# The value and gate projections of layer 1: sums of the next weights ahead of the remainder, one set of copies in smaller buffers, and the following stage's weights handled a product later

## The chip, the cores and the metric

The kernel runs on one core of one Trainium2 chip. The metric is the device time of one execution in microseconds (us). The core has engines that run side by side, each through its own list of instructions in order: TensorE (PE, matrix products), VectorE (DVE), ScalarE (ACT), GpSimd (POOL, hardly used here) and SyncE (SP, which issues nearly all DMA transfers). They wait for one another through semaphores. TensorE's granted clock over the profiled execution is 0.999 of full speed.

## The reference

What is computed is a trunk of two decoder layers on 1024 tokens of width 1024: layer 0 mixes tokens with dilated sliding-window attention, layer 1 with gated linear attention (GLA); each mixer is followed by a squared-ReLU MLP. The change lies in layer 1's mixer, of which this matters:

```python
def gla_mixer(h, w_in, w_gate_up, b_gate, norm_w, w_out):
    proj = h @ w_in
    ...
    q, k, v = proj[..., :s1], proj[..., s1:s2], proj[..., s2:s3]
    g_out, gate_lr = proj[..., s3:s4], proj[..., s4:]
    ...
    gate = jax.nn.silu(g_out.astype(jnp.float32)).reshape(B, S, GLA_HEADS, GLA_DV)
    o = (o * gate).reshape(B, S, GLA_VAL_DIM).astype(h.dtype)
    return o @ w_out
```

`v` and `g_out` are each a product of the normed activations (1024 x 1024) with 1024 columns of `w_in`. The stage in question computes these two products, group 0 being the gate `g_out` with its SiLU, group 1 the values `v`. The stage after it starts with the 16 columns of `gate_lr` and the heads' `k` and `q`.

## The kernel before

**Seven products.** Class `Values` computes a 1024 x 1024 x 1024 product by the Strassen-Winograd scheme: seven products of 512 x 512 blocks instead of eight, on sums and differences of blocks of the activations and of the weights. Each of the seven is done in two halves of 256 rows of the inner dimension. Steps are counted by `n`; for two groups there are 28: `place(n)` gives group g = n // 14, product q = (n % 14) // 2 and half m. "Product n" below is the half product of step n: 24 matmuls of 128 x 128 by 128 x 512 (two blocks of the inner dimension, four blocks of 128 tokens, and three terms). The three terms come from the precision: each operand is split into a rounded part `h` (made by ACT) and a remainder `l` (made by DVE as value minus rounded part), and h·h, h·l and l·h are summed.

**What one step needs.** For the weights of step n: `load(n)` issues a DMA on SP, into a tile named raw, or kept if a later step uses it again; `total(n)` (L784) forms the sum of blocks on DVE where the scheme wants one; `rounded(n)` (L808) is ACT's copy into `dh`; `remain(n)` (L814) is DVE's subtraction into `dl`; `prep(n)` is `rounded` and then `remain`, with `total` ahead where it hasn't been done. For the activations, `hs.sum1` to `hs.sum4` (L350) make sums of blocks on DVE, in two halves of columns c = 0, 1, and `hs.cut` splits them: L344 on ACT and L346 on DVE. `s1` to `s4` are these sums, `a11` to `a22` the blocks themselves.

**What is done with a product.** Products add up in PSUM, in two sets of four banks called A and B; a set that is used afresh (q = 0, 1, 2, 6) has to be free. `sums(n)` does the traffic: at q = 1, 3, 4 and 6 ACT copies the running sum out (`copy`: L896 for group 0, L839 for group 1), at q = 2, 5, 6 and at the next group's q = 0 DVE adds a bank to such a copy (`add`, L844), which finishes one quarter of the result, c11, c12, c21 or c22, each of four tiles t of 128 tokens. The fourth, c21, is copied from A at q = 6 (steps 12 and 13), just ahead of the adds of c22 that read the same banks. For group 1 a finished tile is stored at once (L900). For group 0 it goes on the list `todo`, and SiLU is applied to one tile per step: `begin` (L908, exp on ACT), in the next step `guard` (L913, DVE) and `logs` (L918 and L919, ACT), and in the step after that `close` (L925 to L927, DVE, and the store L928 on SP). `begin` starts at step 7; step 13 has none of the four.

**Buffers.** Tiles share rings by size: `k4`, twenty-five buffers of 4 KB per partition (weights, `dh`, `dl`, halves of the split s2, s3 and s4); `h8`, twelve of 8 KB (among others group 0's copies `gq`, four tiles in one buffer); `t2`, eight of 2 KB; eight PSUM banks. An instruction that takes a buffer waits until the last reader of what stood in it is done, and whatever is behind it on its engine waits too.

**Order.** The order on each engine is that of the calls in `gla_values` (L1729 to L1797), written out by hand for steps 0 to 3, then the loop over n = 4 to 27: first `guard` and `close`, then `sums(n)`, `prep(n + 2)`, loads, `product(n)`, extra cuts, `logs` and `begin`, and `total(n + 3)`.

**The next stage's weights.** They go through `W` (class `Weights`): `W.dma()` issues the next load (L135), `W.prep` splits one (L151 on ACT, L152 on DVE; the 16 columns of `gate_lr`, tile `wboth`, also L158), and `W.pump()` issues loads until four are ahead and prepares up to two of them, within `W.limit`. `plan_gla()` lists them, `wboth` first, at step 22. `wboth` is read by the first matmuls after the stage (L2010).

Of the kernel before, what the change touches and what calls it, by code (L numbers as in the profile page):

```python
# [9 lines left out]
F32 = mybir.dt.float32  # L10
# [3 lines left out]
AF = mybir.ActivationFunctionType  # L14
OP = mybir.AluOpType
# [4 lines left out]
P = 128  # L20
# [21 lines left out]
def hybrid_trunk(ctx, tc, x, norm_mix, norm_mlp, norm_fin, a_in, a_out, g_in, g_up, g_b, g_nw,  # L42
                 g_out, m_up, m_down, tab, msk, gmask, ident_d, out):
    nc = tc.nc
    pe, act, dve, pool, sp = nc.tensor, nc.scalar, nc.vector, nc.gpsimd, nc.sync
# [7 lines left out]
    def h8(shape, dt, name):  # L53
        return wk.tile(shape, dt, name=name, tag="h8", bufs=12)

    def k4(shape, dt, name):
        return wk.tile(shape, dt, name=name, tag="k4", bufs=25)

    def t2(shape, dt, name):
        return wk.tile(shape, dt, name=name, tag="t2", bufs=8)  # L60
# [50 lines left out]
    class Weights:  # L111
        def __init__(self):
            self.slots = []
            self.by = []
            self.ndma = 0
            self.nprep = 0
            self.used = 0
            self.freed = 0
            self.limit = 5
            self.second = dve  # L120
            self.parts = {}
            self.raws = {}
# [57 lines left out]
    W = Weights()  # L180
# [14 lines left out]
    def plan_gla():  # L195
        W.add(cols(g_in, 3072, RANK))
        for h in range(GH):
            add_two(g_in, 512 + DK * h, DK * h)
        for k in range(0, KT, 2):
            add_rows(g_out, k, lambda kt: gnw[:, kt % 2:kt % 2 + 1])  # L200
# [299 lines left out]
    class Up:  # L500
# [100 lines left out]
        def copy(self, p, name):  # L601
            e = t2([P, 512], F32, name)
            act.activation(e, self.st[p]["X"], AF.Copy)
            self.st[p][name] = e
# [273 lines left out]
    class Mixed(Values):  # L878
# [3 lines left out]

        def __init__(self):
            super().__init__()
            self.quad, self.todo, self.open, self.last = {}, deque(), None, None

        def source(self, g):
            return g_in, (2048, 1024)[g]
# [1 line left out]
        def copy(self, name, s, t, g):  # L890
            if g:
                return super().copy(name, s, t, g)
            if t == 0:
                self.quad[name] = h8([P, 4, 512], F32, "gq")
            c = self.c[name, t] = self.quad[name][:, t, :]
            act.activation(c, self.acc[s][t], AF.Copy)  # L896

        def made(self, c, g, rows, cols):
# [2 lines left out]
            else:  # L901
                self.todo.append((c, rows, cols))

        def begin(self):

            if self.todo:
                d = t2([P, 512], F32, "gd")
                act.activation(d, self.todo[0][0], AF.Exp, scale=-1.0)  # L908
                self.open = [*self.todo.popleft(), d]

        def guard(self):
            if self.open is not None:
                dve.tensor_scalar(self.open[3], self.open[3], 1.0, 3e38, op0=OP.add, op1=OP.min)  # L913

        def logs(self):
            if self.open is not None:
                e = t2([P, 512], F32, "ge")
                act.activation(e, self.open[3], AF.Ln)  # L918
                act.activation(e, e, AF.Exp, scale=-1.0)  # L919
                self.last, self.open = [*self.open, e], None  # L920

        def close(self):
            if self.last is not None:
                c, rows, cols, d, e = self.last
                dve.tensor_tensor(d, d, e, op=OP.mult)  # L925
                dve.scalar_tensor_tensor(e, d, 2.0, e, op0=OP.subtract, op1=OP.mult)
                dve.scalar_tensor_tensor(c, c, -1.0, e, op0=OP.mult, op1=OP.mult)  # L927
                sp.dma_start(ggscr[rows, cols], c)  # L928
                self.last = None


    clock = [0]
# [111 lines left out]
    class Heads(Up):  # L1044
# [92 lines left out]
        def follow(self, p, c, points):  # L1137
            h, g = divmod(p, NG)
            a = Attention(g, h, None, None)

            def begin():
                a.qT, a.kT = self.dst.pop((p, 0)), self.dst.pop((p, 1))
            at(c + points[0][0], begin, 0)
            a.plan(c, *points)
# [125 lines left out]
    for p in range(NB // 2):  # L1270
        t = h8([P, 2, D], F32, "x0")
# [9 lines left out]
    hs = Halves(x0, wbc, vals, None)  # L1281
# [117 lines left out]
    for p in range(heads.count):  # L1399
# [3 lines left out]
        if p == heads.count - 1:  # L1403
            for k in range(0, KT, 2):
                add_rows(a_out, k)
            c = 14 * p
# [322 lines left out]
    def gla_values():  # L1729

        hs, m = down.hs, down.mixed
        m.product(0)
        hs.turn(2)
        m.prep(3)
        m.load(4)
        m.product(1, [0, 1])
        m.product(1, [2, 3])
        hs.turn(3)
        m.load(5)
        hs.sum1(0)  # L1740
        hs.cut("s1", 0)
        m.sums(2)
        m.product(2)
        m.prep(4)
        hs.sum1(1)
        hs.cut("s1", 1)
        m.load(6)
        m.sums(3)
        m.product(3)
        m.prep(5)  # L1750
        for c in range(2):
            hs.sum2(c)
        hs.cut("s2", 0)
        m.load(7)
        m.total(6)
        for n in range(4, m.STEPS):
            if n != 13:
                m.guard()
                m.close()
            if n != 5:  # L1760
                m.sums(n)
            if n == 4:
                m.sums(5)
                hs.cut("s2", 1)
            m.prep(n + 2)
            m.load(n + (4 if n < 5 else 5))
            if n == 4:
                m.load(9)
            m.product(n)
            if n == 4:  # L1770
                hs.sum4()
                hs.cut("s4", 0)
            elif n == 5:
                hs.cut("s4", 1)
                hs.sum3()
                hs.cut("s3", 0)
            elif n == 6:
                hs.cut("s3", 1)
                hs.cut("a22", 0)
            elif n == 7:  # L1780
                hs.cut("a22", 1)
            if n != 13:
                m.logs()
                if n >= 7:
                    m.begin()
            if n + 3 < m.STEPS:
                m.total(n + 3)
            if n == 22:
                plan_gla()
                W.limit = 3  # L1790
            if n in (20, 21):
                hs.cut("a21", n - 20)
            if n >= 24:
                W.pump()
        for t in range(4):
            m.add("c21", "B", t, 1)
        return [[m.h["a11"], m.h["a12"]], [m.h["a21"], m.h["a22"]]]  # L1797
# [195 lines left out]

    ol, turn1 = [], []
    hT = gla_values()
    W.take(1)
    AM = k4([P, NB, P], F32, "AM")
# [21 lines left out]
    for h in range(GH):  # L2019
        rows = []  # L2020
# [55 lines left out]
```

## Time and profile before

| | |
|---|---|
| time, median of 3 runs | 2612.7 us (2612.32 to 2613.21) |
| time of the profiled execution | 2613.06 us |
| its span, first to last instruction | 2611.3 us |
| stage of the change in it (product 0 to the first matmul on `wboth`) | 1582.2 to 1743.7 us |

Engines in stretches of that stage, from the view of windows (busy us):

| stretch, us | length | PE | DVE | ACT |
|---|---|---|---|---|
| 1585 to 1618 | 33.0 | 33.00 | 28.53 | 18.45 |
| 1618 to 1636 | 18.0 | 16.09 | 15.71 | 11.12 |
| 1636 to 1662 | 26.0 | 26.00 | 22.74 | 13.51 |
| 1662 to 1700 | 38.0 | 37.82 | 35.52 | 26.02 |
| 1700 to 1745 | 45.0 | 43.82 | 37.36 | 23.58 |

How to read the lines that follow. A line of the timeline gives start and duration in us, engine, line of the kernel, operation, output <- inputs, sizes and count; in brackets stands the idle time of the engine before it and what ended that. A line of the list of waits gives the engine and line that waited, what it waited for, the total in us, how many times, and the longest. Matmuls overlap: each is listed with 0.39 us, while a new one starts every 0.22 to 0.23 us, so time that PE loses is read from the distance between starts.

### The profile page before, as it was taken

Reading aid. Unit: us, or ns where it says so; the run is one execution under the profiler, and the core shown is the slowest. Engines: PE = TensorE matmul, PEld = TensorE weight load, DVE = VectorE, ACT = ScalarE, POOL = GpSimd, SP = SyncE. Lnnn points to the kernel's source line nnn. Section 1 sums busy time; section 2 is a strip of 40 time slices with the busy share of each in tenths; the row PEclk is TensorE's granted clock in tenths of the full one; section 3 lists DMA queues with packets and bytes.
Section 4 is the critical chain, followed back from the end, with each engine's and each line's share of the span. In section 5 each row is a group of like instructions: output and inputs, shape, how many; then the busy total and the mean of one; then the engine's idle time right before and its main releaser. Section 6 shows DMA issues by size and latency. Waiting matters only on the chain.

```text
span 2611.3 us, 33042 instructions
## 1 busy us (share of the span) xinstructions
PE 2586.3 (99%) x12144; PEld 2157.3 (83%) x12144; DVE 1858.9 (71%) x2986; ACT 1276.7 (49%) x2319; POOL 1.8 (0%) x7
## 2 busy tenths in 40 slices
PE   8999999999999999999999999999999999999998
PEld 6888888888888888888888887878888888888887
DVE  7645888888888768666657577977658866666566
ACT  6332455555556446555533345654326545553343
POOL 0000000000000000000000000000000000000000
PEclk9999999999999999999999999999999999999999
DMA  5533465655556733454775452463513544396543
GB/s 190 169 129 124 103 161 131 163 147 150 155 151 183 227 121 128 167 169 137 283 252 185 137 194 93 133 199 97 187 66 123 170 153 157 131 355 200 189 146 125
DMA packets 327010, 423.12 MB, mean 162 GB/s; under 512 B 19808, under 2 KB 192224, under 8 KB 326848
## 3 DMA queue, kind: packets, MB, share of 16 engines
q1 hardware_dynamic: 326848, 421.01, 51.0%
q8 instruction: 95, 1.56, 0.3%
q14 instruction: 67, 0.55, 0.1%
HBM read 279.71 MB, written 116.06 MB: 152 GB/s over the span
## 4 chain that ended last, share of the span: by engine, by line
PE 87%; DVE 8%; ACT 3%; issue 1%; DMA 1%; SPq 0%; ACTq 0%; DVEq 0%
PE pX L598 16%; PE pB L1581 13%; PE pV L598 11%; PE pA L1581 10%; PE pY L598 5%; PE pZ L598 5%; PE pB L829 5%; PE pd L215 3%; PE pd L213 3%; PE pd L214 3%; PE pA L829 3%; PE pO L1017 2%; PE pS L976 2%; PE pP L1003 1%; DVE dl L814 1%
## 5 line engine op out<-in xcount | busy, mean ns | idle before, releaser
L1581 PE MATMUL pB<-dh 128*128 128x512 f32 x512 | 199.4, 389 | 0.0
L1581 PE MATMUL pB<-dh,dl 128*128 128x512 f32 x512 | 199.2, 389 | 0.0
L1581 PE MATMUL pB<-dl,dh 128*128 128x512 f32 x512 | 199.2, 389 | 0.0
L222 DVE TENSOR_TENSOR dl<-sin,dh 128x1024 fp32r<-128x1024 f32 x112 | 136.5, 1218 | 44.6 <-ACT dh L219 44.2
L219 ACT ACTIVATE dh<-sin 128x1024 fp32r<-128x1024 f32 x112 | 117.8, 1052 | 89.7 <-PE pB L1581 32.5
L219 ACT ACTIVATE dh<-kept 128x1024 fp32r<-128x1024 f32 x64 | 67.9, 1061 | 183.4 <-DVE kept L1546 137.8
L598 PE MATMUL pV<-s4h,wd 128*128 128x512 f32 x448 | 150.8, 398 | 0.0
L1581 PE MATMUL pA<-dh,dl 128*128 128x512 f32 x384 | 149.4, 389 | 0.0
L1581 PE MATMUL pA<-dl,dh 128*128 128x512 f32 x384 | 149.4, 389 | 0.0
L1581 PE MATMUL pA<-dh 128*128 128x512 f32 x384 | 149.4, 389 | 0.0
L992 ACT ACTIVATE pt<-pt,orow 128x128 f32<-128x128 f32 (+1 forms) x192 | 84.8, 443 | 96.7 <-DVE orow L990 94.6
L1581 PEld LDWEIGHTS pB<-dh,dl 128*128 128x128 f32 x512 | 96.1, 188 | 20.1
L1581 PEld LDWEIGHTS pB<-dh 128*128 128x128 f32 x512 | 96.1, 188 | 19.9
L1581 PEld LDWEIGHTS pB<-dl,dh 128*128 128x128 f32 x512 | 96.1, 188 | 19.8
L536 DVE TENSOR_TENSOR wal<-raw,wah 128x512 fp32r<-128x512 f32 x112 | 76.2, 686 | 42.9 <-ACT wah L535 42.9
L607 ACT ACTIVATE c<-c 128x512 f32<-128x512 f32 x64 | 40.4, 632 | 122.6 <-DVE c L635 78.9
L598 PEld LDWEIGHTS pV<-s4h,wd 128*128 128x128 f32 x448 | 84.2, 188 | 17.7 <-DVE rb L623 0.2
L222 DVE TENSOR_TENSOR dl<-kept,dh 128x1024 fp32r<-128x1024 f32 x64 | 78.3, 1224 | 25.1 <-ACT dh L219 19.3
L536 DVE TENSOR_TENSOR wbl<-t,wbh 128x1024 fp32r<-128x1024 f32 x56 | 68.6, 1225 | 38.3 <-ACT wbh L535 38.3
L990 DVE CUSTOM_DVE_ANT_0 pt<-pS,masks 128x128 f32<-128x128 f32 (+1 forms) x192 | 58.2, 347 | 51.2 <-PE pS L976 51.2
L598 PE MATMUL pY<-a12h,wah 128*128 128x512 f32 x224 | 89.5, 400 | 0.0
L598 PE MATMUL pZ<-a22h,wgh 128*128 128x512 f32 x224 | 89.3, 399 | 0.0
(336 smaller groups left out, 7364.2 us busy)
## 6 DMA issues: line engine op xcount, KB each, us to landing
sin<-acts SPq DMA_DIRECT2D x112, 512.0 KB, 3.8
raw<-in_mlp_w_up_dram SPq DMA_DIRECT2D x64, 512.0 KB, 6.0
acts<-s SPq DMA_DIRECT2D x64, 512.0 KB, 3.4
raw<-in_mlp_w_down_dram SPq DMA_DIRECT2D x64, 512.0 KB, 4.7
raw<-in_attn_w_in_dram SPq DMA_DIRECT2D x96, 256.0 KB, 4.6
cw<-c SPq DMA_DIRECT2D x192, 128.0 KB, 2.3
acts<-c SPq DMA_DIRECT2D x64, 256.0 KB, 2.1
kept<-in_mlp_w_down_dram SPq DMA_DIRECT2D x32, 512.0 KB, 5.8
```

The lines of the kernel that those rows point to most:

```text
L213: pe.matmul(ps, sh, mh, start=start, stop=False)
L214: pe.matmul(ps, sh, ml, start=False, stop=False)
L215: pe.matmul(ps, sl, mh, start=False, stop=stop)
L219: act.activation(hi, src, AF.Copy)
L222: dve.tensor_tensor(lo, src, hi.bitcast(F32), op=OP.subtract)
L536: self.remain(lambda: dve.tensor_tensor(lo, src, hi.bitcast(F32), op=OP.subtract))
L598: pe.matmul(st[b], u[:, k, :], v, start=first and k + n == 0, stop=k == 3 and n == 2, skip_group_check=True)
L829: pe.matmul(self.acc[s][t], a[:, c], b[:, k, :], start=fresh and m + k + v == 0, stop=m == 1 and k == 1 and v == 2, skip_group_check=True)
L976: pe.matmul(ps[:, i, :128 * n], self.qT[:, 128 * b:128 * b + 128], self.kT[:, k0:k0 + 128 * n], start=True, stop=True)
L990: dve.tensor_tensor_reduce(pt[:, i, :128 * n], ps[:, i, :128 * n], masks[:, m0:m0 + 128 * n], -scale, 1e38, op0=OP.add, op1=OP.min, accum_ ...
L992: act.activation(pt[:, i, :128 * n], pt[:, i, :128 * n], AF.Exp, scale=-1.0, bias=m, accum_out=self.row[:, r, HD:HD + 1])
L1581: pe.matmul(self.acc[s][t], a[:, k, c], b[:, k, :], start=fresh and m + k + v == 0, stop=m == 7 and k == 1 and v == 2, skip_group_check=True)
```

## The change

It has three parts, all in class `Mixed` and in `gla_values`.

1. In the steps written out by hand, `prep(4)` and `prep(5)` are taken apart, and DVE's sums of the next weight (`total`) or of the activations (`sum1`, `sum2`) are called ahead of the remainder.
2. The copies of c21 of group 0 go into two `k4` buffers of two tiles each, instead of one `h8` buffer of four. The state that the SiLU functions hand on is kept in lists; `begin` can take several results, and is called for one.
3. `W.pump()` starts at step 25 instead of 24, two loads are issued by themselves at the end of step 23, and `sums(25)` is called in step 24.

```diff
-            self.quad, self.todo, self.open, self.last = {}, deque(), None, None
+            self.quad, self.todo, self.open, self.last = {}, deque(), [], []
...
         def copy(self, name, s, t, g):
             if g:
                 return super().copy(name, s, t, g)
-            if t == 0:
-                self.quad[name] = h8([P, 4, 512], F32, "gq")
-            c = self.c[name, t] = self.quad[name][:, t, :]
+            if name == "c21":
+                if t % 2 == 0:
+                    self.pair = k4([P, 2, 512], F32, "gp")
+                c = self.c[name, t] = self.pair[:, t % 2, :]
+            else:
+                if t == 0:
+                    self.quad[name] = h8([P, 4, 512], F32, "gq")
+                c = self.c[name, t] = self.quad[name][:, t, :]
             act.activation(c, self.acc[s][t], AF.Copy)
...
-        def begin(self):
-
-            if self.todo:
+        def begin(self, n=1):
+
+            while n and self.todo:
                 d = t2([P, 512], F32, "gd")
                 act.activation(d, self.todo[0][0], AF.Exp, scale=-1.0)
-                self.open = [*self.todo.popleft(), d]
+                self.open.append([*self.todo.popleft(), d])
+                n -= 1
...
         hs.sum1(0)
+        m.total(4)
+        hs.sum1(1)
         hs.cut("s1", 0)
         m.sums(2)
         m.product(2)
-        m.prep(4)
-        hs.sum1(1)
+        m.rounded(4)
+        m.total(5)
+        m.remain(4)
         hs.cut("s1", 1)
         m.load(6)
         m.sums(3)
         m.product(3)
-        m.prep(5)
-        for c in range(2):
-            hs.sum2(c)
+        m.rounded(5)
+        hs.sum2(0)
+        m.remain(5)
+        hs.sum2(1)
         hs.cut("s2", 0)
         m.load(7)
         m.total(6)
...
-            if n != 5:
+            if n not in (5, 25):
                 m.sums(n)
             if n == 4:
                 m.sums(5)
                 hs.cut("s2", 1)
+            if n == 24:
+                m.sums(25)
...
+            if n == 23:
+                W.dma()
+                W.dma()
             if n in (20, 21):
                 hs.cut("a21", n - 20)
-            if n >= 24:
+            if n >= 25:
                 W.pump()
```

More of the change, by code (lines that the diff above doesn't have):

```diff
@@ L902, in made @@
                 self.todo.append((c, rows, cols))
-        def begin(self):
-            if self.todo:
+        def begin(self, n=1):
+            while n and self.todo:
                 d = t2([P, 512], F32, "gd")
                 act.activation(d, self.todo[0][0], AF.Exp, scale=-1.0)
-                self.open = [*self.todo.popleft(), d]
+                self.open.append([*self.todo.popleft(), d])
+                n -= 1
         def guard(self):
-            if self.open is not None:
-                dve.tensor_scalar(self.open[3], self.open[3], 1.0, 3e38, op0=OP.add, op1=OP.min)
+            for o in self.open:
+                dve.tensor_scalar(o[3], o[3], 1.0, 3e38, op0=OP.add, op1=OP.min)
         def logs(self):
-            if self.open is not None:
+            while self.open:
+                o = self.open.pop(0)
                 e = t2([P, 512], F32, "ge")
-                act.activation(e, self.open[3], AF.Ln)
+                act.activation(e, o[3], AF.Ln)
                 act.activation(e, e, AF.Exp, scale=-1.0)
-                self.last, self.open = [*self.open, e], None
+                self.last.append([*o, e])
         def close(self):
-            if self.last is not None:
-                c, rows, cols, d, e = self.last
+            while self.last:
+                c, rows, cols, d, e = self.last.pop(0)
                 dve.tensor_tensor(d, d, e, op=OP.mult)
@@ L928, in close @@
                 sp.dma_start(ggscr[rows, cols], c)
-                self.last = None
     clock = [0]
```

## The prediction

> **What bounds the kernel now.** I read the page first, then the list of waits of TensorE (PE), and then the timeline around each wait.
>
> ```profile
> PE 2586.3 (99%) x12144; PEld 2157.3 (83%) x12144; DVE 1858.9 (71%) x2986; ACT 1276.7 (49%) x2319; POOL 1.8 (0%) x7
> ```
>
> ```profile
> PE pT L334 <- DVE xn L252: 10.4, 7, 8.9
> PE pB L829 <- DVE dl L814: 1.3, 2, 0.8
> PE pB L829 <- DVE c L844: 1.2, 1, 1.2
> PE pA L829 <- DVE dl L814: 0.8, 1, 0.8
> PE pd L215 <- DVE oTl L222: 0.7, 1, 0.7
> ...
> PE pA L829 <- ACT dh L808: 0.4, 1, 0.4
> ```
>
> PE is busy 99% of the span: nothing but its pauses can be won, unless its work becomes less, and the change leaves every matmul as it is. The longest wait (10.4 us on xn) lies outside the stage; of those on L829 all but one of the 1.3 us pair lie in it. "Lost" below is the time between two matmul starts beyond the usual 0.22, which comes out somewhat above the listed wait because PE also restarts.
>
> Three places lose time. **The first** is products 7 and 8 (PE rows, timeline):
>
> ```profile
> 1623.78 0.39 PE L829 MATMUL pA<-dh,s2l 128*128 128x512 f32 x1
> 1624.56 0.49 PE L829 MATMUL pA<-dh,s2h 128*128 128x512 f32 x1 [0.39 <-ACT dh L808]
> 1625.82 0.50 PE L829 MATMUL pA<-dl,s2h 128*128 128x512 f32 x1 [0.76 <-DVE dl L814]
> ...
> 1630.94 0.39 PE L829 MATMUL pA<-dh,s2l 128*128 128x512 f32 x1
> 1631.32 0.50 PE L829 MATMUL pB<-dh,s4h 128*128 128x512 f32 x1
> 1632.58 0.50 PE L829 MATMUL pB<-dl,s4h 128*128 128x512 f32 x1 [0.76 <-DVE dl L814]
> 1632.91 0.40 PE L829 MATMUL pB<-dh,s4l 128*128 128x512 f32 x1
> ```
>
> Product 7 loses 0.55 (0.78 between starts) for the rounded weight and 1.03 (1.26) for its remainder; product 8 loses 0.15, 1.03 and 0.10 (0.33 before the third matmul). Taking the same 0.10 after product 7's restart, that is 2.96 us. From the second matmul of product 7 (1625.82) to its last (1630.94) are 22 starts in 5.12 us, 0.10 of it the restart: 0.228 each, so the 24 matmuls of a product take 5.47. Both wait for a remainder dl, so VectorE (DVE) is the bound here. Its rows show what it does with its time:
>
> ```profile
> 1596.88 1.29 DVE L350 TENSOR_TENSOR s<-a 128x512 f32<-128x512 f32 x2
> ...
> 1599.47 1.22 DVE L784 TENSOR_TENSOR kept<-kept 128x1024 f32<-128x1024 f32 x1
> 1601.82 1.23 DVE L814 TENSOR_TENSOR dl<-kept,dh 128x1024 fp32r<-128x1024 f32 x1 [1.13 <-ACT dh L808]
> ...
> 1607.90 1.23 DVE L814 TENSOR_TENSOR dl<-kept,dh 128x1024 fp32r<-128x1024 f32 x1 [1.13 <-ACT dh L808]
> 1609.05 2.49 DVE L350 TENSOR_TENSOR s<-s,a 128x512 f32<-128x512 f32 x4
> ...
> 1612.66 1.22 DVE L784 TENSOR_TENSOR kept<-raw,kept 128x1024 f32<-128x1024 f32 x1
> ...
> 1622.14 1.21 DVE L784 TENSOR_TENSOR kept<-raw,kept 128x1024 f32<-128x1024 f32 x1
> 1624.54 1.22 DVE L814 TENSOR_TENSOR dl<-kept,dh 128x1024 fp32r<-128x1024 f32 x1 [1.19 <-ACT dh L808]
> ...
> 1631.30 1.23 DVE L814 TENSOR_TENSOR dl<-raw,dh 128x1024 fp32r<-128x1024 f32 x1 [0.86 <-ACT dh L808]
> ```
>
> In each round DVE makes the weight's sum (L784), stands 1.13 us while ScalarE (ACT) rounds it, and only then takes the remainder (L814).
>
> **The second** is product 14 (timeline of all engines; the last line is from the view of the tile gq):
>
> ```profile
> 1659.89 0.34 SPq L928 DMA_DIRECT2D ggscr<-gq  x1
> 1662.18 1.09 ACT L896 ACTIVATE gq<-pA 128x512 f32<-128x512 f32 x2 [6.63 <-issue]
> 1662.81 1.29 DVE L844 TENSOR_TENSOR gq<-pA,gq 128x512 f32<-128x512 f32 x2 [2.95 <-ACT gq L896]
> 1666.38 0.39 PE L829 MATMUL pB<-dl,a12h 128*128 128x512 f32 x1
> 1666.60 0.40 PE L829 MATMUL pB<-dh,a12l 128*128 128x512 f32 x1
> 1667.18 0.50 PE L829 MATMUL pB<-dh,a12h 128*128 128x512 f32 x1 [0.18 <-DVE gq L844]
> DMA to landing us min/median/max: 2.0/2.1/2.8
> ```
>
> ACT stands 6.63 us before the first copy of c21. That copy needs an 8 KB buffer, and the one it gets still holds c11, whose last store is issued at 1659.89 and lands 2.1 later, at 1662.0. DVE's adds of c22 wait behind the copies and PE behind the adds: 0.35 lost, and 0.11 at the restart by the like of product 8.
>
> **The third** is product 26:
>
> ```profile
> 1723.37 3.81 SPq L135 DMA_DIRECT2D raw<-in_gla_w_in_dram  x4
> 1726.00 0.31 ACT L151 ACTIVATE wboth<-raw 128x128 fp32r<-128x128 f32 x1 [4.38 <-DMA raw<-in_gla_w_in_dram]
> 1730.04 1.22 DVE L152 TENSOR_TENSOR wlo<-raw,whi 128x1024 fp32r<-128x1024 f32 x1 [3.40 <-ACT whi L151]
> 1732.41 0.39 PE L829 MATMUL pB<-dh,a22l 128*128 128x512 f32 x1
> 1733.24 1.28 DVE L844 TENSOR_TENSOR c<-pB,c 128x512 f32<-128x512 f32 x2
> 1733.98 0.50 PE L829 MATMUL pB<-dh,a22h 128*128 128x512 f32 x1 [1.18 <-DVE c L844]
> ```
>
> The next stage's weights are issued at 1723.37 and prepared at once; ACT and DVE, which run in order, stand until they land, and with them the adds of sums(25), which free the banks that product 26 writes. PE starts 1.57 after the matmul before: 1.34 lost, with the restart 1.44.
>
> **The change part by part.**
>
> *Sums ahead of the remainder.* Nothing is added or removed; DVE has the next sum or activation sum to do while ACT rounds. From 1596.88 to 1612.66 DVE spends 15.78 us. Its work there is four whole-tile operations at 1.15 (1607.90 to 1609.05) and fourteen halves at 0.60 (six halves between 1609.05 and 1612.66): 4.6 + 8.4 = 13.0. So up to 2.8 us go: the two waits of 1.13 and their edges. For that the moved total(4) must find its weight loaded; it would start at about 1598.1.
>
> ```profile
> 1594.12 0.93 SPq L771 DMA_DIRECT2D kept<-in_gla_w_in_dram  x2
> kept<-in_gla_w_in_dram SPq DMA_DIRECT2D x1, 512.0 KB, 3.7
> ```
>
> Issued at 1594.12 and landing 3.7 later, at 1597.8, it does, by 0.3 us. If that cover fails, the cost is what it is late by. No DMA moves here. ACT's order changes only in that the rounding follows a sum that is now earlier.
>
> Everything behind on DVE up to the remainder of product 7 then comes 2.8 earlier: 1624.54 + 1.22 = 1625.76 becomes 1622.96, before PE's need at about 1624. Product 7 loses nothing. What is late next is product 8: between the remainders of 7 and 8 there are 6.76 us (1624.54 to 1631.30), of which the change removes nothing, and PE needs them 5.47 apart. The remainder of 8 is ready at 1632.53 − 2.8 = 1629.73; product 8 now starts at 1624.0 + 5.47 = 1629.5 at the latest, some 0.1 sooner by the small delay at product 6 that goes too, and wants it a matmul later, at 1629.6. It loses about 0.2, restart counted, and I put 0.3. **Term: 2.96 − 0.3 = 2.7.** If only one of the two waits went (1.4 of the 2.8), product 7 would still lose about 0.4 and product 8 1.3: 1.2 won. If product 8 is in time as well, 3.0. I take 2.7, since every operation in the sum has its row.
>
> *Fourth results in 4 KB pairs.* Four copies keep their size and count; one 8 KB buffer becomes two 4 KB ones, taken at products 12 and 13. Then the copies start when product 11 is done, and DVE's 2.95 goes. **Term: 0.5.** Its ends are 0 (another engine is as late) and 0.5. The lists for begin, guard, logs and close change no instruction, as begin still takes one result per product.
>
> The cost is room among the twenty-five 4 KB buffers: from product 14 on, twelve hold split activations, four the kept weights, two the new pairs. Seven are left for three products' rounded weights and remainders (six) and the loads ahead. So the remainder of product 19 must wait until product 17 ends, where before it did not:
>
> ```profile
> 1686.64 1.22 DVE L814 TENSOR_TENSOR dl<-kept,dh 128x1024 fp32r<-128x1024 f32 x1
> 1687.76 0.39 PE L829 MATMUL pB<-dh,s1h 128*128 128x512 f32 x1
> ```
>
> The second row is product 18's first matmul, so product 17 ends there. A remainder begun then is ready 1.22 later, and product 19 starts 5.47 after it: cover 4.2. Behind the waiting remainder on DVE stand the next sum and the closing of a gate result, on SP the loads ahead, with a cover of several products. Cost taken: nothing; from the other side, 1.1 a product if the buffer came a product later (the third rival).
>
> The Trainium skill has a rule against this part: its page "Perfetto Trace Analysis", section "Identifying Performance Opportunities", says that a gap that repeats on the engine that should be full can mean there is not enough SBUF or PSUM for the next tile. No wait in the list above repeats in this way before the change. By the rows the sum keeps its three terms; by the rule it would be that of the third rival.
>
> *Weights a product later.* Two loads are issued in step 23, ahead of step 24's stores on SP; on SP's row of 3.81 for four issues they delay these by about 1.9, for which nobody waits: the stored values are read by the next stage. The first landed 2.6 after its issue (1723.37 to 1726.00); both now have more than a product's 5.47 before the preparation, which moves from step 24 to 25. sums(25) moves to step 24: two adds (1.28) ahead of the remainder of 26, which has all of product 25 (5.47) to be made in. The preparation falls into steps 25 and 26, when no product waits for DVE except 27, and the adds of c22 no longer free a bank in haste. **Term: 1.4** (0 to 1.44; if the stall moves whole onto product 27's remainder, it is 0).
>
> **Sum:** 2.7 + 0.5 + 1.4 = 4.6 us. The profiled execution took 2613.06 (span 2611.3 and 1.8 around it), so 2608.5 for it; its time is 0.36 above the median of the runs, 2612.7, so the median becomes **2608.1**. Unknown: later stages get other buffers. The only wait of the list after the stage that this could touch is the 0.7 on oTl: 0.7 either way.
>
> **The rivals.**
>
> *All of it goes.* Product 8 is in time too (2.96), with the full 0.46 and 1.44: 4.9; with part of the 0.7 later, 5.3 to 5.6: 2607.1 to 2607.4. For it: 0.3 is all that product 8 lacks. Against: the 6.76 between the remainders.
>
> *Half of it.* The time comes back where the chain stays: product 8 inherits what product 7 gave, or product 27 waits for the weights as 26 did. 1.2 + 0.5 + 0 to 1.4: 2609.6 to 2611.0. For it: DVE's waits of 1.19 and 0.86 before the remainders of 7 and 8 stand in steps that the change leaves as they are.
>
> *Full buffers, slower.* If a remainder gets its buffer only when the product just before its own ends, PE pays a second matmul's wait as at product 8, 1.03 + 0.10, each time; the limit from which it decides is the cover of 4.2 being used up. For products 19 to 22, with ACT's rounding of about 1.06 once in the row, 4.5 + 1.1 = 5.6: net 1.0 slower, 2613.7. If it held through 26, 9.0 + 1.1: net 5.5, 2618.2. Against it: the count gives the buffer at the end of 17, not 18.
>
> **How the numbers follow.** The forecast, 2607.5 to 2609.5, gets 0.52; all of it 0.20; half of it 0.18; full buffers 0.10, half of that within 0.2%. A measurement of this kernel tells about 0.2%, 5.2 us, from no change: that is below 2607.5. So faster 0.20, same 0.75, slower 0.05. The range takes in the first three cases: 2606.8 to 2611.8.
>
> **What would show it.** Right: no wait of 1.13 before L814 near 1600; L829 at product 7 without a wait, at product 8 below 0.3; ACT's 6.63 gone; no wait for c at product 26; DVE waiting before L814 around products 17 to 20 with PE untouched. Wrong: a wait at products 19 to 22 or 27, or product 8 losing over 1 us.

## The result and the profile after

| | before | after |
|---|---|---|
| time, median of 20 runs | 2613.11 us (2612.14 to 2614.64) | 2608.73 us (2608.1 to 2609.42) |
| ratio, 95% interval | | 0.9984 (0.9977 to 0.999) |
| span of the profiled execution | 2611.3 us | 2606.4 us |
| lost between matmul starts, 1588 us to the end of product 27 | 5.42 us | 0.87 us |

The kernel is 4.4 us faster, 0.17%. The interval lies wholly below 1, but the gain is within the 0.2% that count as no change here. The last row sums, over PE's timeline, what each distance between two starts has beyond the usual 0.227 us, where this is over 0.04. It is the sharpest measure in this study. A second profile of the changed kernel has a span of 2607.1, and the 0.7 between the two lies ahead of these products: the first matmul of product 1 starts at 1589.15 in one and at 1589.86 in the other. The sum for the second profile is 0.83.

The first line of the page of the profile and PE's list of waits, after; columns as before:

```profile
PE 2584.3 (99%) x12144; PEld 2157.4 (83%) x12144; DVE 1858.9 (71%) x2986; ACT 1277.0 (49%) x2319; POOL 1.8 (0%) x7
```

```profile
PE pT L334 <- DVE xn L252: 10.4, 7, 8.9
PE pd L215 <- DVE oTl L222: 0.7, 1, 0.7
PE pB L829 <- DVE dl L814: 0.5, 1, 0.5
```

Instruction counts are the same. PE is busy 2.0 us less than before (2586.3), which says nothing, since the second profile of the changed kernel has 2586.4. Of the waits for c, for gq and for weights in the stage none is left in the list: the 0.5 on dl lies in layer 0. DVE's timeline, hand-written steps and the remainders of products 7 and 8, after:

```profile
1596.73 1.29 DVE L350 TENSOR_TENSOR s<-a 128x512 f32<-128x512 f32 x2
1597.94 1.22 DVE L784 TENSOR_TENSOR kept<-kept 128x1024 f32<-128x1024 f32 x1
...
1602.62 1.22 DVE L814 TENSOR_TENSOR dl<-kept,dh 128x1024 fp32r<-128x1024 f32 x1
...
1606.16 1.22 DVE L814 TENSOR_TENSOR dl<-kept,dh 128x1024 fp32r<-128x1024 f32 x1
...
1609.71 1.22 DVE L784 TENSOR_TENSOR kept<-raw,kept 128x1024 f32<-128x1024 f32 x1
...
1621.60 1.23 DVE L814 TENSOR_TENSOR dl<-kept,dh 128x1024 fp32r<-128x1024 f32 x1 [1.19 <-ACT dh L808]
...
1628.36 1.23 DVE L814 TENSOR_TENSOR dl<-raw,dh 128x1024 fp32r<-128x1024 f32 x1 [0.85 <-ACT dh L808]
```

From the first row to the sum at 1609.71 are 12.98 us instead of 15.78; the two brackets of 1.13 are gone, and those of 1.19 and 0.85 stand, 6.76 apart, as they were. What is left of product 8's loss, on PE:

```profile
1629.13 0.39 PE L829 MATMUL pB<-dh,s4h 128*128 128x512 f32 x1
1629.64 0.50 PE L829 MATMUL pB<-dl,s4h 128*128 128x512 f32 x1
1629.97 0.39 PE L829 MATMUL pB<-dh,s4l 128*128 128x512 f32 x1
```

The starts are 0.51 and 0.33 apart: 0.28 and 0.10 are lost here, and 0.05 some matmuls on. Product 12 loses 0.26 (0.19 before), and no other distance in the stage loses more than 0.09. The first copy of c21, for which ACT stood 6.63 us before, on ACT's timeline after:

```profile
1652.54 1.07 ACT L901 ACTIVATE gp<-pA 128x512 f32<-128x512 f32 x2
```

It has no wait ahead of it and starts in product 12 (1651.37 to 1656.89) instead of product 13. The price in buffers, in the timelines of DVE and of ACT, after:

```profile
1684.36 1.23 DVE L814 TENSOR_TENSOR dl<-kept,dh 128x1024 fp32r<-128x1024 f32 x1 [5.10 <-PE pA L829]
...
1701.70 1.23 DVE L814 TENSOR_TENSOR dl<-raw,dh 128x1024 fp32r<-128x1024 f32 x1 [2.01 <-DMA ggscr<-gq]
```

```profile
1700.61 1.06 ACT L808 ACTIVATE dh<-raw 128x1024 fp32r<-128x1024 f32 x1 [4.12 <-PE pA L829]
```

The remainder of product 19 stands 5.10 us for the end of product 17, and the rounding for product 22 stands 4.12 for the end of product 20. The remainder behind that rounding stands 2.01; the profile puts this down to a store, but the rounding that it reads also ended only at 1701.67. PE loses nothing there. The tail, by the same two engines and SP's queue, after:

```profile
1718.87 1.14 SPq L135 DMA_DIRECT2D raw<-in_gla_w_in_dram  x2
```

```profile
1723.01 2.48 DVE L844 TENSOR_TENSOR c<-pB,c 128x512 f32<-128x512 f32 x4
```

The first weights are issued in step 23, and sums(24) and sums(25) are four adds in a row. Afterwards ACT still stands 1.31 us for a later load (issued at 1730.59), and DVE 1.74 us for ACT's part in splitting a weight. By then the remainder of product 27, the last of the stage, has been started (1729.72), so no product needs either.

### The profile page after: what moved, and what is told of

It is laid out like the page before. It is cut to its first block, busy times and chain, and to the rows that moved or that the text cites. A ratio compares the mean times of both kernels' runs of the same rounds, so it can differ in the third digit from the quotient of the medians.

```text
span 2606.4 us, 33046 instructions
## 1 busy us (share of the span) xinstructions
PE 2584.3 (99%) x12144; PEld 2157.4 (83%) x12144; DVE 1858.9 (71%) x2986; ACT 1277.0 (49%) x2319; POOL 1.8 (0%) x7
## 4 chain that ended last, share of the span: by engine, by line
PE 95%; DVE 3%; ACT 1%; issue 0%; DMA 0%; SPq 0%; ACTq 0%; DVEq 0%
PE pX L598 18%; PE pB L1587 13%; PE pV L598 12%; PE pA L1587 10%; PE pB L829 7%; PE pY L598 6%; PE pZ L598 6%; PE pA L829 5%; PE pd L215 3%; PE pd L213 3%; PE pd L214 3%; PE pO L1023 2%; PE pS L982 2%; PE pP L1009 1%; PE pT L334 1%; DVE dl L814 1%
```

## The experiments

The question is whether each part ended its own stall, as the prediction adds them up, or whether they hang together. The table has what PE lost in each run by place, in us, from starts as above, each from one profile. Columns 26, 27 and 19 to 21 include the slow matmuls after a wait; the total also has 0.17 at the starts of products 1 and 2, the same in every run. Behind it stand the median of the run and that of the kernel before, taken beside it.

| kernel | 6 to 8 | 12 | 14 | 19 to 21 | 26, 27 | all | median | before | ratio, 95% interval |
|---|---|---|---|---|---|---|---|---|---|
| before | 3.12 | 0.19 | 0.46 | 0 | 1.44 | 5.42 | | | |
| after | 0.43 | 0.26 | 0 | 0 | 0 | 0.87 | 2608.73 | 2613.11 | 0.9984 (0.9977 to 0.999) |
| sums alone | 0.44 | 0.19 | 0.47 | 0 | 1.05 | 2.35 | 2610.55 | 2613.24 | 0.9991 (0.9981 to 1.0) |
| pairs alone | 3.18 | 0.23 | 0 | 0 | 7.39 | 11.03 | 2619.51 | 2613.24 | 1.0025 (1.0015 to 1.0034) |
| tail alone | 3.08 | 0.23 | 0.47 | 0 | 0 | 4.00 | 2611.89 | 2613.24 | 0.9995 (0.9986 to 1.0004) |
| all but the pairs | 0.42 | 0.23 | 0.42 | 0 | 0 | 1.26 | 2609.4 | 2613.24 | 0.9986 (0.9976 to 0.9995) |
| pairs, adds early | 3.14 | 0.24 | 0 | 0 | 6.94 | 10.58 | 2617.98 | 2613.37 | 1.0016 (1.0005 to 1.0028) |
| pairs, weights later | 3.21 | 0.24 | 0 | 0 | 0.17 | 3.83 | 2612.16 | 2613.37 | 0.9995 (0.9984 to 1.0006) |
| adds early alone | 3.19 | 0.25 | 0.41 | 0 | 0 | 4.06 | 2612.34 | 2613.31 | 0.9996 (0.9986 to 1.0006) |
| after, one buffer held | 0.44 | 0.24 | 0 | 0.20 | 0 | 1.09 | 2609.72 | 2613.37 | 0.9986 (0.9974 to 0.9997) |
| after, two held | 0.45 | 0.25 | 0 | 8.2 | 0 | 9.10 | 2617.77 | 2613.37 | 1.0018 (1.0006 to 1.0029) |

**Sums alone.** The kernel before with part 1:

```diff
         hs.sum1(0)
+        m.total(4)
+        hs.sum1(1)
         hs.cut("s1", 0)
...
-        m.prep(4)
-        hs.sum1(1)
+        m.rounded(4)
+        m.total(5)
+        m.remain(4)
...
-        m.prep(5)
-        for c in range(2):
-            hs.sum2(c)
+        m.rounded(5)
+        hs.sum2(0)
+        m.remain(5)
+        hs.sum2(1)
```

> Part one alone (the sums ahead of the remainders in the hand-written steps before the loop), before otherwise unchanged. Theory (each stall is ended by its own part, and the gains add): the two waits of 1.13 on VectorE near 1600 us go, product 7 has no wait, product 8 loses about 0.4; the stalls at product 14 (0.46 lost) and product 26 (1.44 lost) stay as they were. Gain 2.6 to 2.8 us: span about 2608.6, time about 2610.4. Rival (the gain is handed back, the chain behind it stays): product 14 or 26 loses more than before by what was won, gain under 1.5 us.

Measured: 2.68 us less lost at products 6 to 8, and 0.39 less at product 26, for a median 2.7 lower. The gain isn't handed back. The 0.39 was not foreseen. The traces show where it lies, in ACT's stand for the second of the next stage's weights, before and in this run:

```profile
1728.95 1.06 ACT L151 ACTIVATE whi<-raw 128x1024 fp32r<-128x1024 f32 x1 [1.55 <-DMA raw<-in_gla_w_in_dram]
```

```profile
1725.67 1.06 ACT L151 ACTIVATE whi<-raw 128x1024 fp32r<-128x1024 f32 x1 [1.15 <-DMA raw<-in_gla_w_in_dram]
```

SP took 3.81 us for the four issues before and 3.21 here. The runs below that issue the four weights in a row as well took 3.22, 3.83 and 2.89 (pairs alone, pairs with the adds early, adds early alone), so the 0.39 isn't shown to come from the sums; it may be a difference between two profiles.

**Pairs alone.** The kernel before with part 2:

```diff
+            if name == "c21":
+                if t % 2 == 0:
+                    self.pair = k4([P, 2, 512], F32, "gp")
+                c = self.c[name, t] = self.pair[:, t % 2, :]
...
```

> Only the fourth result (c21) in two 4 KB buffers instead of one of 8 KB; order of sums and weights as before. Theory: ScalarE's idle 6.63 us before the first copy of c21 goes, product 14 loses 0 instead of 0.46; products 7 and 8 (2.96) and 26 (1.44) lose as before; the remainder of product 19 waits for the end of product 17, with TensorE untouched. Gain 0.4 to 0.5 us: span about 2610.8. Rival (the 4 KB buffers are too few): TensorE waits for a remainder or a rounded weight in products 19 to 22, a loss of 1 us or more, span 2612 or above.

Measured: 6.3 us slower. Neither expectation holds as written: product 14's loss goes, and products 19 to 22 lose nothing; the loss is at product 26. PE, DVE, ACT and SP's queue in four timelines of this run:

```profile
1732.18 0.39 PE L829 MATMUL pB<-dh,a22l 128*128 128x512 f32 x1
1738.27 0.79 PE L829 MATMUL pB<-dh,a22h 128*128 128x512 f32 x1 [5.71 <-DVE c L844]
```

```profile
1687.57 1.23 DVE L814 TENSOR_TENSOR dl<-kept,dh 128x1024 fp32r<-128x1024 f32 x1 [5.10 <-PE pA L829]
...
1704.91 1.23 DVE L814 TENSOR_TENSOR dl<-raw,dh 128x1024 fp32r<-128x1024 f32 x1 [2.01 <-DMA ggscr<-gq]
...
1734.34 1.23 DVE L152 TENSOR_TENSOR wlo<-raw,whi 128x1024 fp32r<-128x1024 f32 x1 [3.09 <-ACT whi L151]
```

```profile
1703.82 1.06 ACT L808 ACTIVATE dh<-raw 128x1024 fp32r<-128x1024 f32 x1 [4.12 <-PE pA L829]
```

```profile
1727.93 3.22 SPq L135 DMA_DIRECT2D raw<-in_gla_w_in_dram  x4
```

The rounding and the remainder of product 22 in the kernel before, on ACT and on DVE:

```profile
1698.61 1.06 ACT L808 ACTIVATE dh<-raw 128x1024 fp32r<-128x1024 f32 x1
```

```profile
1701.87 1.22 DVE L814 TENSOR_TENSOR dl<-raw,dh 128x1024 fp32r<-128x1024 f32 x1
```

The remainder of product 19 began at 1686.64 and now begins at 1687.57, 0.93 later. The rounding of product 22 now stands for the end of product 20 and begins 5.21 later, and the remainder behind it, at 1704.91, 3.0 later. The issue of the weights comes at 1727.93 instead of 1723.37, 4.56 later. PE itself is 0.2 us *ahead* at product 26 (1732.18 against 1732.41). So the buffers made DVE, ACT and SP late step by step, and each product still got its weights in time; the lateness stayed on these engines until the one place that had no cover left, where DVE stood for the next stage's weights and with it the adds that product 26 needs. The wait of 1.18 became 5.71.

**Tail alone.** The kernel before with part 3:

```diff
-            if n != 5:
+            if n not in (5, 25):
                 m.sums(n)
...
+            if n == 24:
+                m.sums(25)
...
+            if n == 23:
+                W.dma()
+                W.dma()
...
-            if n >= 24:
+            if n >= 25:
                 W.pump()
```

> Only part three: sums(25) in step 24, the first two loads of the next stage's weights in step 23, their preparation from step 25 on. Theory: the wait of 1.18 for c at product 26 goes and nothing takes its place, products 7, 8 and 14 lose as before: gain 1.4 us, span about 2609.9. Rival (the stall moves to the remainder of product 27): gain under 0.5 us and a wait on dl at product 27.

Measured: product 26 loses 0 instead of 1.44, product 27 nothing; the median is 1.35 lower, with an interval that includes no change. The theory's size stands by the starts.

**All but the pairs.** The changed kernel with c21 in its 8 KB buffer, and the SiLU functions as they were.

```diff
-            if name == "c21":
-                if t % 2 == 0:
-                    self.pair = k4([P, 2, 512], F32, "gp")
-                c = self.c[name, t] = self.pair[:, t % 2, :]
-            else:
-                if t == 0:
-                    self.quad[name] = h8([P, 4, 512], F32, "gq")
-                c = self.c[name, t] = self.quad[name][:, t, :]
+            if t == 0:
+                self.quad[name] = h8([P, 4, 512], F32, "gq")
+            c = self.c[name, t] = self.quad[name][:, t, :]
...
```

> Parts one and three, c21 in its 8 KB buffer as before. Theory: gain 4.2 to 4.4 us (span about 2606.9), product 14 loses 0.46 again, and VectorE does not stand some 5 us before the remainder of product 19, because two 4 KB buffers more are free. Rival (full 4 KB buffers cost TensorE something that the trace hides): without the pairs the kernel is no slower than with them, span 2606.4 or less.

Measured: 4.16 us less lost than before, product 14's 0.42 back, and on DVE no wait for a buffer before the remainder of product 19. On top of the other two parts the pairs are worth 0.39 of lost time (1.26 less 0.87), where the prediction gave them 0.5; alone they cost 6.3. The next two runs ask which half of part 3 turns them.

**Pairs with the adds early.** The pairs, and `sums(25)` in step 24; weights as before.

```diff
+            if name == "c21":
...
-            if n != 5:
+            if n not in (5, 25):
                 m.sums(n)
...
+            if n == 24:
+                m.sums(25)
```

> The pairs with sums(25) moved to step 24; the weights of the next stage loaded and prepared in step 24 as before. With the pairs alone VectorE, ScalarE and SyncE run 4.6 us later against TensorE by step 24 (SyncE's first weight load 1727.93 instead of 1723.37), and the stand for the weights that cost 1.18 at product 26 costs 5.71. Theory (two delays on one chain, and the adds are what product 26 needs of it): product 26 no longer waits for c, but the remainder of product 27 is still behind the stand for the weights, so that product 27 loses 1 to 3 us: span 2611 to 2613. Rival (moving the adds is all that was needed): no wait after product 14, span about 2609.5.

Measured: product 27 is the place that the theory named, but the loss is over twice its upper end of 3 us, and the span of 2616.5 lies above its 2613. Product 26 loses nothing and product 27 loses 6.94. PE's timeline, the first two rows and the two at the end of the slow stretch:

```profile
1737.20 0.50 PE L829 MATMUL pB<-dh,a22h 128*128 128x512 f32 x1 [0.64 <-ACT dh L808]
1740.71 0.79 PE L829 MATMUL pB<-dl,a22h 128*128 128x512 f32 x1 [3.01 <-DVE dl L814]
...
1746.42 0.53 PE L829 MATMUL pB<-dh,a22l 128*128 128x512 f32 x1
1746.79 0.40 PE L829 MATMUL pB<-dh,a22h 128*128 128x512 f32 x1
```

The waits cost 0.80 and 3.28, and the 14 distances from 1740.71 to 1746.79 are 0.43 on average instead of 0.227: another 2.9. That second price stood in no expectation.

**Pairs with the weights later.** The pairs, two loads in step 23, `W.pump()` from step 25; `sums(25)` in its old step.

```diff
+            if name == "c21":
...
+            if n == 23:
+                W.dma()
+                W.dma()
...
-            if n >= 24:
+            if n >= 25:
                 W.pump()
```

> The pairs with the weights of the next stage issued in step 23 and prepared from step 25; sums(25) in step 25 as before. Theory (the stand for the weights in step 24 is what the 4.6 us of lateness by full buffers fall on): without it the adds of sums(25) begin at about 1729.7, ready a microsecond before product 26 wants the bank at 1732.4, so product 26 loses less than 0.4, products 7 and 8 lose 2.96 as before: span about 2609.5. Rival (the late buffers delay the adds by themselves): a wait for c at product 26 of over 1 us remains.

Measured: 0.17 lost at product 26, and this row of DVE:

```profile
1731.68 1.28 DVE L844 TENSOR_TENSOR c<-pB,c 128x512 f32<-128x512 f32 x2
```

The adds begin at 1731.68, not at 1729.7 as expected (the closing of a gate result stands ahead of them), and just in time. The engines are as late as with the pairs alone (the remainder of product 22 begins at 1704.86, there at 1704.91); only the stand for the weights has left step 24, and 7.2 of the 7.39 go with it. With the run before, this shows that moving the weights is what makes the pairs free, and that moving the adds alone doesn't.

**Adds early alone.** The kernel before with the two edits of `sums(25)` and nothing else.

```diff
-            if n != 5:
+            if n not in (5, 25):
                 m.sums(n)
...
+            if n == 24:
+                m.sums(25)
```

> The kernel before with nothing changed but sums(25) moved to step 24 (no pairs, weights loaded and prepared in step 24). With the pairs this left product 27 some 4.1 us late (0.80 and 3.28 lost), the side engines there being 4.6 us later against TensorE. Theory (two delays on one chain): without the pairs the remainder of product 27 is in time by about half a microsecond, products 26 and 27 lose under 0.4 together: span about 2610, gain 1.1 to 1.4 us. Rival (the stand for the weights costs product 27 even so): a wait on a rounded weight or a remainder at product 27 of over 1 us.

Measured: products 26 and 27 lose nothing. The remainder of product 27 is made here by:

```profile
1735.47 1.22 DVE L814 TENSOR_TENSOR dl<-raw,dh 128x1024 fp32r<-128x1024 f32 x1
```

It is ready at 1736.69, 0.9 us before product 27 starts (1737.59). So without the pairs the adds alone remove the 1.44; with them they don't, and the edit that was enough for one delay isn't for two.

**How many buffers are left.** The changed kernel with small 4 KB tiles written in step 12 and again in step 25, which hold one buffer each:

```diff
+            if n == 12:
+                pads = [k4([P, 2, 512], F32, "pad") for _ in range(1)]
+                for t in pads:
+                    dve.tensor_copy(t[:, 0, 0:4], bgate)
+            if n == 25:
+                for t in pads:
+                    dve.tensor_copy(t[:, 0, 4:8], t[:, 0, 0:4])
             if n not in (5, 25):
```

> The changed kernel with one more 4 KB buffer held idle from step 12 to step 25 (two tiny copies write it; nothing reads it). Theory (the changed kernel still has cover): the remainders of products 18 to 22 wait longer on VectorE, TensorE loses under 0.3 us, span 2606.3 to 2607. Rival (the cover is nearly used up): waits for a remainder or a rounded weight in products 18 to 27, 1 us or more.

The same with `range(2)`:

> As before with two such buffers held. Theory: with two buffers fewer a remainder gets its buffer only when the product just before its own ends; TensorE then waits at the second matmul of a product, about 1.1 us each time for products 19 to 24, 4 to 8 us in all, span 2610 to 2615. Rival (cover is left even then): span under 2608.

Measured: one buffer less costs PE 0.20 (in product 20), under the 0.3 expected (the span of 2608.2 is above the expected 2607, but this run enters product 0 at 1583.60, 1.6 later than the changed kernel); two cost 8.2, a little over its 4 to 8, and in three products, not six. PE's list of waits and DVE's timeline, two held:

```profile
PE pA L829 <- DVE c L844: 2.7, 1, 2.7
PE pA L829 <- DVE dl L814: 1.9, 2, 0.9
PE pB L829 <- DVE dl L814: 1.5, 2, 0.9
```

```profile
1689.94 1.22 DVE L814 TENSOR_TENSOR dl<-kept,dh 128x1024 fp32r<-128x1024 f32 x1 [5.11 <-PE pB L829]
...
1696.61 1.22 DVE L814 TENSOR_TENSOR dl<-kept,dh 128x1024 fp32r<-128x1024 f32 x1 [0.72 <-PE pB L829]
...
1707.86 1.23 DVE L814 TENSOR_TENSOR dl<-kept,dh 128x1024 fp32r<-128x1024 f32 x1 [5.30 <-PE pA L829]
```

Products 19, 20 and 21 each lose 1.09 at their second matmul and 0.11 at the next, because the remainder starts when the product just before ends. That is the mechanism of the third rival, at 1.20 each instead of its 1.13. What it hadn't is the 2.69 wait for c in product 20, behind the late remainder on DVE, with slow matmuls after it.

**Two attempts to do better.** The changed kernel with the weight of product 8 rounded and its remainder made in step 5, and then also with the adds of step 11 first in that step:

```diff
                 hs.cut("s4", 1)
+                m.prep(8)
                 hs.sum3()
...
-            m.prep(n + 2)
+            if n != 6:
+                m.prep(n + 2)
...
-            if n + 3 < m.STEPS:
+            if n != 5 and n + 3 < m.STEPS:
                 m.total(n + 3)
```

> The changed kernel with the rounding and remainder of product 8 made in step 5 ahead of the activation sum sum3 (they stood in step 6). Theory (product 8 loses its 0.4 us because VectorE makes sum3 and more ahead of that remainder): the loss at product 8 goes, no other appears, 0.4 us below the changed kernel. Rival (sum3 or its split is late instead): a wait on an activation or a later remainder of 0.4 us or more.

```diff
+            if n == 11:
+                m.sums(n)
             if n != 13:
                 m.guard()
                 m.close()
-            if n not in (5, 25):
+            if n not in (5, 11, 25):
                 m.sums(n)
```

> As the one before, and the adds of step 11 ahead of the closing of the gate result in that step. Theory: product 12's 0.26 us go as well, since a bank is free sooner: 0.6 to 0.7 us below the changed kernel, no lost time above 0.1 at a start left in the stage. Rival: the closing is then late and holds up a store or a buffer, visible as a new wait.

Beside them the changed kernel again:

> The changed kernel itself, beside the others on one chip: 2608.7 us as before, TensorE losing 1.0 us between products 3 and 26.

Measured against the kernel before, 2613.31: 2608.91 for the first (0.9984, 0.9975 to 0.9993), 2608.98 for the second (0.9984, 0.9975 to 0.9993), 2608.94 for the changed kernel (0.9983, 0.9974 to 0.9992). PE lost 1.00, 0.81 and 0.83. The 0.43 at the start of product 8 goes in both, and about 0.65 comes some matmuls on, so the theory's gain of 0.4 fails and the rival's loss is there; PE, first attempt:

```profile
1631.15 0.39 PE L829 MATMUL pB<-dh,s4l 128*128 128x512 f32 x1
1631.92 0.50 PE L829 MATMUL pB<-dh,s4h 128*128 128x512 f32 x1 [0.39 <-ACT gq L901]
```

The activation sum that now stands behind the remainder comes 1.3 later on DVE (1625.96 against 1624.65 in the changed kernel beside it). With it come, on ACT, the split that waits for it, 1.3 later (1627.27 against 1625.96), and the copy that frees product 8's next bank, 0.4 later (1631.27 against 1630.91). The second attempt also wins product 12's loss. Neither time differs from the changed kernel's.

## Why the prediction was right

**Sums, 2.7 us.** Products 6 to 8 lose 2.69 less, and DVE's stretch is shorter by 2.80. Load 4 was in time: there is no wait before the sum at 1597.94. Product 8 keeps 0.43 where I put 0.3: it starts at 1629.13, and its remainder is ready only at 1629.59.

**Pairs, 0.5 us.** Product 14's 0.46 goes. The wait for the end of product 17 came where the count put it, 5.10 us long, and PE had cover. But the step "Cost taken: nothing" holds only beside part 3. I followed the wait as far as the next product and not along DVE, ACT and SP to step 24, where it arrives as 4.56 us on the stand for the weights. The pairs alone would have cost 6.3 where the prediction's term says 0.5 gained; that the terms simply add was an assumption, right for this sum and wrong for this part. Part 3 was put in for the stall at product 26, and nothing in the prediction says that the pairs need it; that it stood in the same change was luck for the forecast.

**Weights later and adds early, 1.4 us.** Product 26's 1.44 goes, and nothing waits at product 27. It has two edits. Without the pairs the adds alone remove the stall; whether the weights alone do was not run. With the pairs the adds alone don't, and the weights alone leave 0.17.

**The sum.** 2.69 + 0.46 + 1.44 − 0.07 (product 12) is 4.5 of lost time; 4.4 is the change of the median, 4.6 was forecast. The forecast time, 2608.1, is 0.6 below the measured one; 0.4 of that is the median of the kernel before, 2612.7 in three runs and 2613.11 in twenty.

**The rivals.** *Half of it*: product 8 didn't inherit what product 7 gave, and nothing came back at product 27. *All of it*: product 8 is still late. *Full buffers*: the changed kernel is two buffers away from it. The pairs without part 3 are slower too, but at another place and by another mechanism, lateness that adds up until step 24. The rule of the Trainium skill weighed in the prediction ("Perfetto Trace Analysis", section "Identifying Performance Opportunities", a repeating gap as a sign of too little SBUF) describes the run with two buffers held: 1.09 lost three times, a product apart. It doesn't show the shortage that the changed kernel has, which leaves no gap on PE.

## What to carry to other kernels

A wait that TensorE doesn't feel isn't yet free: follow the lateness along the engines that have it, until they next stand for something else, because there the two add up. Parts of a change that meet on one such chain can't be priced one by one; take each alone and all but each. And where a fix needs buffers, find out how many are left by holding some back: here the second one held cost 8 us and the first 0.2.

## What was not expected of the hardware

After a long enough wait TensorE ran slow. The view of windows, with granted clock after the five busy times, two buffers held and then pairs with the adds early:

```profile
1690.00:1698.00 8.00, 6.13 (x27) 4.54 (x26) 7.21 (x10) 2.74 (x4) 0.00 (x0) 1.00 0.50 166
...
1702.00:1706.00 4.00, 3.98 (x10) 3.12 (x11) 0.56 (x1) 0.00 (x0) 0.00 (x0) 0.57 0.52 197
```

```profile
1741.00:1747.00 6.00, 6.00 (x15) 4.68 (x15) 3.20 (x6) 0.00 (x0) 0.00 (x0) 0.52 1.06 309
```

The granted clock is 1.00 where waits of about 0.94 us come (1690 to 1698) and 0.57 and 0.52 after waits of 2.69 and 3.01 us; the matmuls then start every 0.43 us for 3.75 and 6.08 us, which costs 1.7 and 2.9 us on top of the wait. After the 5.71 of the pairs alone the slow stretch lasted 3.14 us and cost 1.5. The longest pause of the stage without it is the 1.57 between starts at product 26 of the kernel before. Where the limit lies is open: ahead of the 2.69 stand two pauses of 1.32 between starts within 11 us, and no run shows whether they had a share in it. The Trainium skill's page "TensorE: Matmul & The Clock Gate", section "Part 1: The HAM clock gate (the "warmup" mystery)", says that TensorE falls to half clock after an idle window of about 3.4 us and comes back after as long a busy one, with windows that run freely. The half rate agrees with the trace: 0.43 us between starts instead of 0.227. The wait of 2.69 us, after which it came, is shorter than that idle window, and the slow stretches here lasted from 3.14 to 6.08 us.
